# Splitting the last store, moving the last wait to Pool and making do with 14 fewer semaphores in a streaming matrix-vector kernel

## The chip, the cores and the metric

One core of one Trainium2 chip. The metric is the device time of one execution in microseconds (us). The engines are called PE (TensorE, the matrix engine), DVE (VectorE), ACT (ScalarE), Pool (GpSimd) and SyncE. A semaphore is a counter on which engines wait. The traces show a DMA increment one behind its data: in the profiled run of before, the last store's packets ended at 627.520 us, and the last eight increments of its semaphore came from 627.618 to 627.870. A single run of this kernel varies by some 0.2 to 0.3 us (one standard deviation) around its mean.

## The reference

```python
def reference(x, w):                       # x: (8, 2048, 4096) fp32, w: (4096, 1)
    proj = (x @ w).squeeze(-1)             # 8 x 2048
    cm = np.maximum.accumulate(proj, axis=1)
    is_record = (proj >= cm).astype(np.float32)
    return np.cumsum(is_record, axis=1).astype(np.float32)
```

268 MB are read and 64 KB written.

## The kernel before

SyncE issues all loads of x. DVE multiplies and sums 2816 of the 4096 columns of a row, Pool and ACT the other 1280, PE turns the sums into rows of a PSUM tile, and DVE scans them: running maximum, comparison, running count. The sequence of 2048 is done in groups of 512, 512, 512 and 384, and the last 128 positions in a finer tail. The counts stand in `cnt`: one row for each of 8 batches, so partitions 0 to 7.

The parts that matter here:

```python
    xs = [sem("xs") for _ in range(B)]
    fr = [sem("fr") for _ in range(B)]
    xq = [sem("xq") for _ in TILES]                      # 13, one for each load of the tail
    ws, bw, wc, cs, ..., go, ..., ml = (sem(n) for n in ...)   # 19 more
    # ... the loads of the tail: 13 DMAs on SyncE, each .then_inc(xq[i], 16)
    # ... dot(...)._wait_ge(xq[i], 16); G.tensor_mul(...)._wait_ge(xq[i], 16)
        tail_scans(3, 4, 10)                             # the last scan, .then_inc(cs, 1)
        SY.dma_start(out=out[:, STARTS[-1] :], in_=cnt)._wait_ge(cs, NG + 4).then_inc(
            oe, 16
        )
        A.wait_ge(oe, 16)
```

The last store carries 512 columns: 384 of the last group, which are ready some 20 us earlier, and the tail's 128. At the end of the program, outside the kernel's own code, SyncE collects a signal from every engine (its last instruction of this at 628.140 us in the profiled run of before), a barrier follows, Pool clears a range of semaphores (628.627 to 628.958, with records for 54 of them), and a second barrier ends it (629.253).

Of the kernel before, what the change touches and what calls it, by code (L numbers as in the profile page):

```python
# [20 lines left out]
def kernel(  # L21
# [17 lines left out]
    B, S, D = x.shape  # L39
    WC = 512  # L40
    NW = D // WC
# [3 lines left out]
    NG = len(RS)  # L45
    NL = NG - 1
    N = R * P
    STARTS = [sum(RS[:g]) * P for g in range(NG)]
    S0 = sum(RS) * P
# [18 lines left out]
    def rows_of(m):  # L68
        return m * H % B, m * H // B * Q

    TILES = [(m, 0, D, (0, VC), (VC, D)) for m in range(B - 2)] + LAST
# [7 lines left out]
    def sb(shape, name, **kw):  # L79
        return pool.tile(shape, FP32, name=name, **kw)  # L80
# [8 lines left out]
    cnt = sb([B, N], "cnt")  # L89
# [21 lines left out]
    def sem(name):  # L111
        return tc.alloc_semaphore(f"{name}_{next(ns)}")

    xs = [sem("xs") for _ in range(B)]
    fr = [sem("fr") for _ in range(B)]
    xq = [sem("xq") for _ in TILES]
    ws, bw, wc, cs, od, oe, psr, pd, pl, go, sd, pa, con, fo, ms, p7, mg, pg, ml = (
        sem(n) for n in "ws bw wc cs od oe psr pd pl go sd pa con fo ms p7 mg pg ml".split()
    )

    V, A, G, T, SY = nc.vector, nc.scalar, nc.gpsimd, nc.tensor, nc.sync

    def dot(xsl, wsl, dst, seed=0.0):
        return V.tensor_tensor_reduce(  # L124
            out=xsl, in0=xsl, in1=wsl, scale=1.0, scalar=seed,
            op0=ALU.mult, op1=ALU.add, accum_out=dst,
        )

    def add_up(xsl, dst):
        return A.activation(out=xsl, in_=xsl, func=ACTF.Copy, accum_out=dst)  # L130

    def w_pool(c0, c1):
        if c0 >= VC:
            return w_sb[:, c0 - VC : c1 - VC]
        assert W2 <= c0 and c1 <= W2 + W2C
        return w2[:, c0 - W2 : c1 - W2]
# [13 lines left out]
    def at(g, t):  # L150
        return xbuf[(t if g < NL else t + NS - 1) % NS]

    def user_before(g, t):
        if t >= NS:
            return t - NS, g + 1
        if g == NL:
            return B - NS + t, g
        return max(u for u in range(B) if u % NS == t), g

    def free(u, n):  # L160
        return (p7, n) if u == B - 1 else (fr[u], 2 * n)

    with tc.tile_critical(no_gpsimd_drain=True):

        for g in range(NG):
            r = RS[g]
            for t in range(B):
                i = SY.dma_start(
                    out=at(g, t)[:, : r * D],
                    in_=x[B - 1 - t, STARTS[g] : STARTS[g] + r * P, :].rearrange(  # L170
                        "(p r) d -> p (r d)", r=r
                    ),
                ).then_inc(xs[t], 16)
                u, n = user_before(g, t)
                if n:
                    i._wait_ge(*(free(u, n)))
                if g == t == 0:
                    A.dma_start(
                        out=w_row, in_=w.rearrange("(k c) one -> k (c one)", k=NW)
                    ).then_inc(ws, 16)  # L180
                if t == 4 and g:
                    SY.dma_start(
                        out=out[:, STARTS[g - 1] : STARTS[g]], in_=cnt
                    )._wait_ge(cs, g + 1).then_inc(od, 16)

        def slot(m):
            if m < NS:
                return None, xbuf[m][:, RS[-1] * D :]
            u = B - NS if m < 2 * NS else B - NS + 1
            return u, at(NL, u)[:, (m % NS) * D : (m % NS + 1) * D]  # L190
# [3 lines left out]
        for i, (m, c0, c1, _, _) in enumerate(TILES):  # L194
            u, xb = slot(m)
            d = SY.dma_start(  # L196
                out=xb[:, c0:c1],
                in_=x[
                    rows_of(m)[0] : rows_of(m)[0] + H,
                    S0 + rows_of(m)[1] : S0 + rows_of(m)[1] + Q, c0:c1,  # L200
                ].rearrange("b i d -> i b d"),
            ).then_inc(xq[i], 16)
            if u not in freed:
                freed.add(u)
                d._wait_ge(*free(u, NG))
# [4 lines left out]
            out=identity, in_=identity, compare_op=ALU.not_equal, fill=1.0,  # L210
# [10 lines left out]
        for n, k in enumerate(order):  # L221
            c = k * WC
            dst = w_v[:, c : c + WC] if c < CV else ps
            i = T.matmul(  # L224
                out=dst, lhsT=identity[:NW, k : k + 1].to_broadcast([NW, P]),
                rhs=w_row, start=True, stop=True,
            ).then_inc(bw, 1)
# [11 lines left out]
            out=by_b, in_=identity.rearrange("p (i b) -> p b i", b=H),  # L239
# [3 lines left out]
            out=by_i, in_=identity.rearrange("p (i b) -> p i b", b=H), op=ALU.add,  # L243
# [82 lines left out]
        def sums(i, dst_v, dst_p, seed=0.0):  # L326
            nonlocal nv, npool, na
            m, _, _, v, p = TILES[i]
            xb = slot(m)[1]
            dot(xb[:, v[0] : v[1]], w_v[:, v[0] : v[1]], dst_v, seed)._wait_ge(  # L330
                xq[i], 16
            ).then_inc(sd, 1)
            nv += 1
            if p:
                xl = xb[:, p[0] : p[1]]
                G.tensor_mul(out=xl, in0=xl, in1=w_pool(*p))._wait_ge(  # L336
                    xq[i], 16
                ).then_inc(pl, 1)
                npool += 1
                add_up(xl, dst_p)._wait_ge(pl, npool).then_inc(pa, 1)  # L340
                na += 1
# [20 lines left out]
        def tail_scans(k0, k1, base):  # L362
            c = S0 - STARTS[-1]
            a, b = k0 * Q, k1 * Q
            scans(
                cm[:, c + a : c + b], cnt[:, c + a : c + b], ps[:B, a:b],
                cm[:, c + a - 1 : c + a], cnt[:, c + a - 1 : c + a], base,
            )

        for m in range(B - 2):  # L370
            k = m // 2
            v, p = acc_v[:, m : m + 1], acc_p[:, m : m + 1]
            sums(m, v, p)
            pick_a(col(2 * k, m), p)
            pick(G, col(2 * k + 1, m), v)._wait_ge(sd, nv).then_inc(mg, 1)
            if m == 2:
                group_scans(RS[-1])
            if m == 4:
                tail_scans(0, 2, 4)
            if m % 2:  # L380
                if k != 1:
                    T.wait_ge(cs, NG + 1 + k // 2)
                turn(2 * k, k, True, False)._wait_ge(ms, m + 1)
                mm = turn(2 * k + 1, k, False, True)._wait_ge(mg, m + 1)
                if k:
                    mm.then_inc(psr, 1)

        npart = [0, 0]
        for i in range(B - 2, len(TILES)):
            n = i - (B - 2)  # L390
            m, p = TILES[i][0], TILES[i][4]
            z = m - (B - 2)
            v, dp = part_v[:, n : n + 1], part_p[:, n : n + 1]
            s = SEED[n]
            if s is not None:
                V.wait_ge(sd, B - 2 + s + 1)
            sums(i, v, dp, 0.0 if s is None else part_v[:, s : s + 1])
            if p:
                pick_a(col(6 + npart[z], m), dp)
                npart[z] += 1  # L400
            if n in (1, len(LAST) - 2):
                pick(G, col(8, m), v)._wait_ge(sd, nv).then_inc(mg, 1)
            if n == 1:
                tail_scans(2, 3, 7)
# [5 lines left out]
        turn(8, 3, False, False)._wait_ge(mg, B)  # L410
        turn(9, 3, False, True)._wait_ge(ml, 1).then_inc(psr, 1)
        tail_scans(3, 4, 10)
        SY.dma_start(out=out[:, STARTS[-1] :], in_=cnt)._wait_ge(cs, NG + 4).then_inc(
            oe, 16
        )
        A.wait_ge(oe, 16)


# [28 lines left out]
```

## Time and profile before

| | before |
|---|---|
| time, first set | 630.23 us median of 3 (630.13 to 630.26) |
| DMA | 427 GB/s over the span, busy almost throughout |
| engines busy | DVE 65%, Pool 59%, ACT 29%, PE 5% |
| last store issued, in the profiled run | 626.394 us |
| end of the span | 629.253 us |

The profile shows a DMA row of 9s in 39 of 40 slices, and the engines wait for the loads: 181.8 us of idle time ahead of DVE's sums and 243.3 us ahead of Pool's products end on them. So I take the kernel as bound by its loads, and what lies ahead of the first load and behind the last one is left. The lines that carry this stand in the prediction below. I call the time from the issue of the last store to the end of the span the *tail end*: 629.253 - 626.394 = 2.859 us.

### The profile page before, as it was taken

The numbers are of one execution on the slowest core, as the hardware profiler recorded it, in microseconds if no ns is written. First come the engines' busy times: TensorE is split into PE (matmuls) and PEld (weight loads), VectorE is DVE, ScalarE is ACT, GpSimd is POOL, SyncE is SP. The second block draws the span as 40 slices with busy tenths as digits, with TensorE's granted clock in tenths as the row PEclk, the third lists the DMA queues.
The fourth block names the chain that finished last, engine by engine and source line by source line (L and its number), as shares of the span: only waits on it lengthen the run. The fifth ranks groups of instructions, "written<-read, shape, count | busy, mean of one in ns | idle before, by whom it ended". The sixth has DMA issues, their size and how long they took to land. (4 is left out here: it accounts for less than half of the span.)

```text
span 629.3 us, 1140 instructions
## 1 busy us (share of the span) xinstructions
PE 29.1 (5%) x96; PEld 13.5 (2%) x96; DVE 407.3 (65%) x294; ACT 181.2 (29%) x274; POOL 370.7 (59%) x149
## 2 busy tenths in 40 slices
PE   8000000000020000000001000000002000000100
PEld 3000000000010000000000000000001000000000
DVE  0755775556766567755578655676556976655897
ACT  1222332223322233222233222332223232232254
POOL 0554675456765557745577555676557666555775
PEclk9999999999999999999996555555555555555565
DMA  9999999999999999999999999999999999999996
GB/s 401 400 467 400 446 421 425 442 437 429 442 425 450 417 450 417 459 408 458 408 458 408 458 408 458 408 459 408 462 418 438 416 447 441 413 447 444 404 425 248
DMA packets 6563, 268.54 MB, mean 427 GB/s; under 512 B 760, under 2 KB 1016, under 8 KB 1568
## 3 DMA queue, kind: packets, MB, share of 16 engines
q1 hardware_dynamic: 6544, 268.50, 98.9%
q10 hardware_dynamic: 16, 0.02, 0.0%
q14 instruction: 3, 0.02, 0.0%
HBM read 268.45 MB, written 0.07 MB: 427 GB/s over the span
## 5 line engine op out<-in xcount | busy, mean ns | idle before, releaser
L124 DVE CUSTOM_DVE_ANT_0 xall<-xall,w_v 128x2816 f32<-128x2816 f32 (+1 forms) x129 | 385.5, 3041 | 181.8 <-DMA xall<-in_x_dram 181.8
L276 POOL TENSOR_TENSOR xall<-xall,w_sb 128x1280 f32<-128x1280 f32 x120 | 345.0, 2909 | 246.7 <-DMA xall<-in_x_dram 243.3
L130 ACT ACTIVATE xall<-xall 128x1280 f32<-128x1280 f32 (+2 forms) x130 | 162.9, 1253 | 428.6 <-POOL xall L276 408.3
L312 PE MATMUL ps<-identity,small 128*8 128x128 f32 x60 | 13.0, 406 | 568.6 <-PEq L309 568.6
L130 ACT ACTIVATION_READ_ACCUMULATOR xall<-xall 128x1 f32 x130 | 24.2, 186 | 0.0
L336 POOL TENSOR_TENSOR xall<-xall,w_sb 128x1280 f32<-128x1280 f32 (+2 forms) x8 | 21.1, 2632 | 3.1 <-DMA xall<-in_x_dram 3.0
L312 PEld LDWEIGHTS ps<-identity,small 128*8 128x8 f32 x60 | 7.3, 125 | 575.4 <-issue 571.3
L140 DVE TENSOR_TENSOR_SCAN cm<-ps,cm,small 8x512 f32<-8x512 f32 (+3 forms) x8 | 7.0, 869 | 18.8 <-PE ps L312 18.4
L224 PE MATMUL w_v<-w,identity 8*128 8x512 f32 x14 | 12.1, 1056 | 0.0
L124 DVE DVE_READ_ACCUMULATOR2_ANT small<- 128x1 f32 x133 | 10.8, 81 | 0.0
L246 DVE MEMSET ps<- 8x512 f32 x1 | 0.5, 485 | 15.7 <-ACT w L235 15.7
L146 DVE TENSOR_TENSOR_SCAN cnt<-ps,cnt,small 8x512 f32<-8x512 f32 (+3 forms) x8 | 7.0, 870 | 0.3
L224 PEld LDWEIGHTS w_v<-w,identity 8*128 8x128 f32 x14 | 4.6, 332 | 7.3 <-issue 7.3
L143 DVE TENSOR_TENSOR ps<-ps,cm 8x512 f32<-8x512 f32 (+3 forms) x8 | 3.9, 487 | 0.3
L232 ACT COPY w_sb<-w_v 128x768 f32<-128x768 f32 x1 | 0.8, 799 | 11.4 <-PE w_v L224 11.4
L347 POOL TENSOR_TENSOR masked<-fold,small 128x4 f32<-128x4 f32 x8 | 1.6, 201 | 3.2 <-DVE small L124 3.2
L124 DVE CUSTOM_DVE_ANT_0 xall<-xall,w_v,small 128x480 f32<-128x480 f32 (+2 forms) x4 | 3.1, 810 | 0.2 <-DVE small L124 0.2
L357 PE MATMUL ps<-fold,masked 128*8 128x32 f32 x20 | 2.0, 235 | 25.3 <-ACT masked L352 17.7
L352 ACT ACTIVATE masked<-fold,small 128x4 f32<-128x4 f32 x10 | 3.0, 298 | 0.3
L336 POOL TENSOR_TENSOR xall<-xall,w 128x640 f32<-128x640 f32 (+1 forms) x2 | 2.3, 1137 | 0.1
L224 PE MATMUL ps<-w,identity 8*128 8x512 f32 x2 | 2.1, 1135 | 2.6 <-DMA w<-in_w_dram 2.6
L231 ACT ACT_TABLE_LOAD x1 | 1.3, 1283 | 2.7 <-DVE fold L242 2.7
(18 smaller groups left out, 5.3 us busy)
## 6 DMA issues: line engine op xcount, KB each, us to landing
xall<-in_x_dram SPq DMA_DIRECT2D x8, 6144.0 KB, 33.5
xall<-in_x_dram SPq DMA_DIRECT2D x6, 2048.0 KB, 42.4
xall<-in_x_dram SPq DMA_DIRECT2D x1, 1264.0 KB, 36.6
xall<-in_x_dram SPq DMA_DIRECT2D x1, 816.0 KB, 39.3
xall<-in_x_dram SPq DMA_DIRECT2D x1, 784.0 KB, 37.9
xall<-in_x_dram SPq DMA_DIRECT2D x2, 240.0 KB, 26.6
xall<-in_x_dram SPq DMA_DIRECT2D x1, 416.0 KB, 39.4
xall<-in_x_dram SPq DMA_DIRECT2D x24, 45.0
```

The costliest lines, as they stand in the source:

```text
L124: return V.tensor_tensor_reduce(out=xsl, in0=xsl, in1=wsl, scale=1.0, scalar=seed, op0=ALU.mult, op1=ALU.add, accum_out=dst,)
L130: return A.activation(out=xsl, in_=xsl, func=ACTF.Copy, accum_out=dst)
L140: V.tensor_tensor_scan(out=cm_, data0=src, data1=low, initial=cm0, op0=ALU.max, op1=ALU.max,)._wait_ge(psr, base).then_inc(psr, 1)
L143: V.tensor_tensor(out=src, in0=src, in1=cm_, op=ALU.is_ge)._wait_ge(psr, base + 1).then_inc(psr, 1)
L146: V.tensor_tensor_scan(out=cnt_, data0=src, data1=low, initial=cnt0, op0=ALU.add, op1=ALU.max,)._wait_ge(psr, base + 2).then_inc(cs, 1)
L224: i = T.matmul(out=dst, lhsT=identity[:NW, k : k + 1].to_broadcast([NW, P]), rhs=w_row, start=True, stop=True,).then_inc(bw, 1)
L276: i = G.tensor_mul(out=xl, in0=xl, in1=w_sb).then_inc(pl, 1)
L312: i = T.matmul(out=ps[:B, j : r * P : r], lhsT=l[:, j * B : (j + 1) * B], rhs=identity, start=k == 0, stop=k == 1,)
L336: G.tensor_mul(out=xl, in0=xl, in1=w_pool(*p))._wait_ge(xq[i], 16).then_inc(pl, 1)
L347: return eng.tensor_tensor(out=e, in0=by_b, in1=acc.to_broadcast([P, H]), op=ALU.mult)
L352: return A.activation(out=e, in_=by_b, func=ACTF.Copy, scale=acc)._wait_ge(pa, na).then_inc(ms, 1)
L357: return T.matmul(out=ps[:B, k * Q : (k + 1) * Q], lhsT=masked[:, n * B : (n + 1) * B], rhs=by_i, start=start, stop=stop,)
```

## The change

The intent is to shorten that tail end in three ways. The group's 384 columns get a store of their own, issued behind the last load; only the tail's 512 bytes a row are left for the end. Pool instead of ACT waits for the stores, with an increment of a semaphore nobody waits for any more. The tail's 13 loads signal on semaphores that other parts are done with, and the unused `go` is dropped, so that 14 fewer exist.

```diff
-    xq = [sem("xq") for _ in TILES]
-    ws, bw, wc, cs, od, oe, psr, pd, pl, go, sd, pa, con, fo, ms, p7, mg, pg, ml = (
+    ws, bw, wc, cs, od, oe, psr, pd, pl, sd, pa, con, fo, ms, p7, mg, pg, ml = (
...
+    xq = [(ws, 32), (bw, NW + 16), (wc, 3 + 16), (con, 7 + 16), (fo, 1 + 16)]
+    xq += [(s, 32) for s in xs[:5]] + [(s, 2 * NG + 16) for s in fr[:3]]
...
-            ).then_inc(xq[i], 16)
+            ).then_inc(xq[i][0], 16)
...                                      # the two waits on xq[i] take *xq[i]
-        SY.dma_start(out=out[:, STARTS[-1] :], in_=cnt)._wait_ge(cs, NG + 4).then_inc(
-            oe, 16
-        )
-        A.wait_ge(oe, 16)
+        for a, b, n in ((STARTS[-1], S0, 1), (S0, S, 4)):
+            SY.dma_start(
+                out=out[:, a:b], in_=cnt[:, a - STARTS[-1] : b - STARTS[-1]]
+            )._wait_ge(cs, NG + n).then_inc(oe, 16)
+        G.wait_ge(oe, 32).then_inc(ml, 1)
```

More of the change, by code (lines that the diff above doesn't have):

```diff
@@ L115 @@
     fr = [sem("fr") for _ in range(B)]
-    xq = [sem("xq") for _ in TILES]
-    ws, bw, wc, cs, od, oe, psr, pd, pl, go, sd, pa, con, fo, ms, p7, mg, pg, ml = (
-        sem(n) for n in "ws bw wc cs od oe psr pd pl go sd pa con fo ms p7 mg pg ml".split()
-    )
+    ws, bw, wc, cs, od, oe, psr, pd, pl, sd, pa, con, fo, ms, p7, mg, pg, ml = (
+        sem(n) for n in "ws bw wc cs od oe psr pd pl sd pa con fo ms p7 mg pg ml".split()
+    )
+    xq = [(ws, 32), (bw, NW + 16), (wc, 3 + 16), (con, 7 + 16), (fo, 1 + 16)]
+    xq += [(s, 32) for s in xs[:5]] + [(s, 2 * NG + 16) for s in fr[:3]]
     V, A, G, T, SY = nc.vector, nc.scalar, nc.gpsimd, nc.tensor, nc.sync
@@ L330, in sums @@
             dot(xb[:, v[0] : v[1]], w_v[:, v[0] : v[1]], dst_v, seed)._wait_ge(
-                xq[i], 16
+                *xq[i]
             ).then_inc(sd, 1)
@@ L336, in sums @@
                 G.tensor_mul(out=xl, in0=xl, in1=w_pool(*p))._wait_ge(
-                    xq[i], 16
+                    *xq[i]
                 ).then_inc(pl, 1)
```

## The prediction

> **What bounds the kernel now.** I read the page first, then the chain that ended last in order of time, then the timeline and the waits of the last 30 us, and last the semaphore records behind the final instruction, because the change touches nothing else.
>
> ```profile
> DMA  9999999999999999999999999999999999999996
> HBM read 268.45 MB, written 0.07 MB: 427 GB/s over the span
> ```
>
> Over 39 of the 40 slices the 16 DMA engines are at least 90% busy with loading x. The kernel is bound by its loads; a change that neither adds nor removes loads can only act in front of the first or behind the last one. The same shows in stages:
>
> ```profile
> 604.50:622.00 17.50, 1.14 (x12) 0.64 (x12) 15.66 (x19) 7.78 (x18) 13.68 (x10) 0.50 0.99 419
> 622.00:626.40 4.40, 0.87 (x8) 0.41 (x8) 3.90 (x14) 1.97 (x7) 1.82 (x3) 0.50 0.21 81
> 626.40:629.30 2.90, 0.00 (x0) 0.00 (x0) 0.00 (x0) 0.00 (x0) 0.00 (x0) 0.50 0.03 6
> ```
>
> Each line is a window in us with the busy time of PE, PEld, DVE, ACT and Pool, then granted clock, DMA share and GB/s. Until 622 the DMA share is 0.99; for 4.4 us the last sums and scans run; in the last 2.9 us no engine computes at all. Those 2.9 us are where this change must earn what it earns. The end of the chain, and what the queue of SyncE waited for:
>
> ```profile
> 581.81 39.25 DMA xall<-in_x_dram
> 621.06 0.07 issue
> 621.13 1.76 POOL xall L336
> ...
> 626.10 0.27 DVE cnt L146
> ```
> ```profile
> 604.68 1.00 DVE L146 TENSOR_TENSOR_SCAN cnt<-ps,cnt,small 8x384 f32<-8x384 f32 x1
> ...
> 626.39 0.32 SPq L413 DMA_DIRECT2D out_dram<-cnt  x1
> ```
> ```profile
> SPq L413 <- DVE cnt L146: 21.8, 1, 21.8
> ```
>
> 384 of the 512 columns that the last store carries are ready at 604.68 + 1.00 = 605.68, but their store waits until 626.39 for the tail's last scan; SyncE sits idle 21.8 us. Behind the store stand only waits and the clean-up:
>
> ```profile
> L163 ACTq COMPARE_BRANCH  x1: 37/37/37, 627.9 to 627.9; - x1
> L163 ACTq DRAIN  x1: 8/8/8, 628.1 to 628.1; - x1
> L163 SPq NOP  x1: 13/13/13, 628.1 to 628.1; - x1
> ```
> ```profile
> L442 POOLq EVENT_SEMAPHORE_RANGE_CLEAR  x1: 331/331/331, 628.6 to 628.6; - x1
> L442 POOLq EVENT_SEMAPHORE  x4: 17/17/17, 628.3 to 629.1; - x4
> ```
>
> ACT holds the wait for the store (a branch that waits), then tells SyncE, whose NOP closes the collection; Pool then clears the range of semaphores in 331 ns, and a second barrier ends the program at 629.25.
>
> The trace's own records give these steps to the nanosecond. Issue 626.394 (319 ns); eight data packets of 2048 bytes from 627.183 to 627.520, which took 107, 227, 234, 111, 233, 211, 81 and 81 ns; increments of the store's semaphore: one at 626.872, eight from 627.618 to 627.870. ACT's branch 627.891, its drain 628.062, SyncE's NOP 628.140, clear 628.627 to 628.958, last semaphore instruction ended 629.253. So: store 1.476 us (626.394 to 627.870), hand-over 0.270 us (627.870 to 628.140), barrier before the clear 0.487, clear 0.331, rest 0.295.
>
> [...] This store is issued by SyncE, not GpSimd; here the receipt part is 627.870 - 627.520 = 0.35 us and issue to first packet is 0.79 us, so the larger piece lies in front of the data. Either way bytes are the small part of 1.476 us.
> [...]
> [...] SyncE's last load issue ends at 604.54 by the timeline; no run yet shows a store behind the tail loads.
> [...] ACT's waiting branch to ACT's next instruction is 171 ns, of which 37 are recorded, while two successive semaphore instructions of Pool start 78 ns apart (628.310 and 628.388).
>
> **The change part by part.**
> (1) Two stores for one. The first, 8 x 1536 bytes, needs the group's scan (605.68) and is issued about 605.7, in SyncE's idle time. A 2048-byte packet of the three earlier stores took 84 ns under full load, so this one is about 65 ns on each of eight engines, behind the last load, whose packets end at 622.9 (623.75 on the slowest engine). It should land by about 624.2, over 3 us before the second. On the path: 0. The second store has 512 instead of 2048 bytes a row. Load packets of 1920 and 3328 bytes took 79 and 131 ns, so 0.037 ns a byte; 1536 bytes fewer is 57 ns. The packets of 211 to 234 ns carry some 140 ns that isn't bytes at this rate; I leave it in place. Worth -57 ns; -130 if the slow packets shrink in proportion.
> (2) The wait moves from ACT to Pool, and the built program shows how. On ACT the wait sits on the branch that leaves the critical part. On Pool it increments a semaphore, so it stays an instruction of its own, and the branch behind it has no wait; such branches leave no record in this trace (Pool, DVE and PE have none at the place of ACT's). New path: landing, about 21 ns to Pool's wait (as ACT's, 627.870 to 627.891), 78 ns to Pool's NOP, about 22 for its increment (626.802 to 626.824), about 20 until SyncE's NOP, which is the last of SyncE's collecting instructions and waits for Pool alone. ACT was collected one instruction earlier; that hop goes. Sum 141 ns for 270: -129 ns. Pool's drain of 41 ns moves behind its NOP, but the barrier needs SyncE's increment 146 ns after SyncE's NOP (628.140 to 628.286), so it stays hidden.
> (3) The 13 semaphores of the tail's loads (one for each entry of the list of tail tiles, 6 + 7) and the unused `go` are no longer made: 14 fewer. The clear covered 48 of the kernel's and 6 of the frame's, 54, as its records count; after, 40. Its records run from 628.648 to 628.930, 5.3 ns each; 14 x 5.3 = 74. Clear 331 to 257: -74 ns.
> (4) The reused semaphores change only the numbers waited for: no instruction, no order. The instruction order agrees on all engines but for one more store on SyncE and Pool's wait. 0.
> Sum: -57 - 129 - 74 = -260 ns; 630.23 - 0.26 = 629.97 us, 0.04%.
>
> **The rivals.**
> A: the early store collides with the last loads and pushes the tail. For it: those loads do set the chain (39.25 us of it)[...]. Against it: [...] even wholly in front it adds only 65 ns to eight engines. It would give 630.0 to 630.1.
> B: the store is latency alone: fewer bytes save nothing, or the smaller row pays the same slow packets. For it: 0.79 and 0.35 us of 1.476 are not data, and half of the packets were slow while nothing else ran. Then 630.03.
> C: Pool's hand-over isn't shorter, because its branch costs something though unrecorded, as ACT's does (171 against 78 ns). Then (2) gives about -40 (the hop alone), 630.06.
> D: a wait on a reused semaphore ends late or early, and the tail's DVE or Pool stalls. The counts are exact multiples reached before the tail's landings, and the race check passes; it would show as idle time from 604 on. Under 5% for me; some us.
> A gain of 2% would be 12.6 us, four times the whole idle end.
>
> **Range and chances.** The parts together can give from -0.1 (B and C) to -0.35 (slow packets shrink), so 629.88 to 630.13. Three runs of before spread over 0.13, and its profiled run took 631.05; another session can shift by some tenths. I say 629.96, with 629.65 to 630.2 for 8 in 10. Within 2%: 0.99; faster and slower 0.005 each.
>
> **What would show it.** (1) A store issue at about 605.7, and a last one at 626.4 with packets of 512 bytes that end some 60 ns sooner. (2) No waiting branch on ACT; landing to SyncE's NOP about 140 ns. (3) A clear of about 257 ns. All engines' rows until 626.4 as before. A last load landing later, or a span that shrinks by over 0.4 us or not at all, would make me wrong in mechanism, though hardly in the verdict.

The forecast's sum came to -57 - 129 - 74 = -260 ns. That the early store would come behind the loads was the assumption. The "about 20" of part (2) is an estimate that names no source; the trace after has 17 ns there.

## The result, and the profile after

The changed kernel took 629.65 us (median of 4, 629.52 to 629.75), before 630.25 (median of 4, 630.13 to 630.47). The ratio is 0.999 with a 95% interval from 0.9973 to 1.0007. A ratio here is the mean time of one kernel's runs over that of the other's of the same rounds, so not quite the ratio of the medians. The interval holds 1: these eight runs alone don't show a gain. The medians differ by 0.60 us where I had said 0.26, and 629.65 lies at the very edge of my range. By the 2% line it is the same, as predicted; the size was wrong.

First the loads and the end of the chain, in order of time (start, length, what):

```profile
580.85 39.27 DMA xall<-in_x_dram
620.12 0.07 issue
620.19 1.76 POOL xall L338
...
625.14 0.27 DVE cnt L148
```

All of it comes 0.96 us earlier than before, but no part is shorter: 39.27 us of loads for 39.25, and 625.14 - 580.85 = 44.29 for 626.10 - 581.81 = 44.29. So the early store did not disturb the loads, and the 0.96 arose far ahead of anything that was changed: the chain's first piece, at 483 us, already comes 0.96 us earlier. The profiled run of before had taken 631.05 us, slower than its others; one must not read a gain from two single spans.

Stages after, in windows as for before (us, busy time of PE, PEld, DVE, ACT and Pool, granted clock, DMA share, GB/s):

```profile
622.00:625.43 3.43, 0.86 (x8) 0.41 (x8) 2.93 (x12) 1.87 (x6) 0.93 (x2) 0.50 0.04 14
625.43:627.80 2.37, 0.00 (x0) 0.00 (x0) 0.00 (x0) 0.00 (x0) 0.00 (x0) 0.50 0.01 2
```

The stretch in which nothing computes has shrunk from 2.9 to 2.4 us. Its parts, first the queue of SyncE, then the collection, then the clear:

```profile
604.76 20.97 SPq L416 DMA_DIRECT2D out_dram<-cnt  x2
```
```profile
L165 ACTq DRAIN  x1: 8/8/8, 625.8 to 625.8; - x1
...
L165 POOLq NOP  x1: 13/13/13, 626.8 to 626.8; - x1
L165 SPq NOP  x1: 13/13/13, 626.8 to 626.8; - x1
```
```profile
L445 POOLq DRAIN  x3: 34/41/103, 626.9 to 627.6; - x3
L445 POOLq EVENT_SEMAPHORE_RANGE_CLEAR  x1: 248/248/248, 627.3 to 627.3; - x1
```

Two stores now share one line of this answer, from 604.76 to the end of the second's issue. The early store's own issue took 3.10 us, against 0.30 of the last one; SyncE had nothing else to do. ACT is through its part at 625.8, 0.4 us after the start of the last store's issue for 1.7 before, Pool's NOP is the last to be collected, and the clear has fallen from 331 to 248 ns. The trace's records, in ns (the store runs from the start of its issue to the last increment of its semaphore; the NOP is SyncE's last instruction of the collection; the rest is the second barrier):

| | before | after | difference | predicted |
|---|---|---|---|---|
| last store, issue to last increment | 1476 | 1235 | -241 | -57 |
| hand-over, increment to SyncE's NOP | 270 | 165 | -105 | -129 |
| barrier, NOP to clear | 487 | 460 | -27 | 0 |
| clear | 331 | 248 | -83 | -74 |
| rest | 295 | 295 | 0 | 0 |
| tail end | 2859 | 2403 | -456 | -260 |

The early store's packets started 17.0 to 18.0 us after its issue, the last of them at 622.808, where the last packet of the loads had ended at 622.806: it did wait for the loads, as the prediction had assumed. Its last increment came at 623.336, 2.1 us ahead of the last store's issue. So 0.46 of the 0.60 us are accounted for by the tail end, the store is the large miss, and 0.14 us are open. The experiments go to these two.

### The profile page after: what moved, and what is told of

Its sections match the earlier page's. It is cut to its first block, busy times and chain, and to the rows that moved or that the text cites. A ratio compares the mean times of both kernels' runs of the same rounds, so it can differ in the third digit from the quotient of the medians.

```text
span 627.8 us, 1141 instructions
## 1 busy us (share of the span) xinstructions
PE 29.4 (5%) x96; PEld 13.6 (2%) x96; DVE 407.2 (65%) x294; ACT 181.1 (29%) x274; POOL 370.5 (59%) x149
```

## The experiments

All numbers of a tail end are ns from the run's own trace. Times are means of five runs against the nine of before in the same set, unless said otherwise.

### Each part alone, and all together

The store alone, with the wait left on ACT's branch:

```diff
-        SY.dma_start(out=out[:, STARTS[-1] :], in_=cnt)._wait_ge(cs, NG + 4).then_inc(oe, 16)
-        A.wait_ge(oe, 16)
+        for a, b, n in ((STARTS[-1], S0, 1), (S0, S, 4)):
+            SY.dma_start(out=out[:, a:b], in_=cnt[...])._wait_ge(cs, NG + n).then_inc(oe, 16)
+        A.wait_ge(oe, 32)
```

> Only the split of the last store; the wait stays on ACT's branch, the semaphores stay 54. Theory S (the eight rows of a store share one rate of about 48 GB/s, as 16384 bytes in 0.337 us before and 4096 in 0.086 after say): last issue to last increment falls from 1.476 to about 1.24 us, time -0.24 us against before. Theory P of the prediction (each packet pays its own 0.037 ns a byte): -0.06, at most -0.13. Hand-over stays 0.27 us and the clear 331 ns under both.

The wait alone:

```diff
-        A.wait_ge(oe, 16)
+        G.wait_ge(oe, 16).then_inc(ml, 1)
```

> Only the wait moved to Pool, with its increment; one store of 2048 bytes a row, 54 semaphores. Prediction: landing to SyncE's NOP 0.141 us for 0.270, time -0.13; the changed kernel's trace had 0.165, so -0.11 is the better guess. Rival C (Pool's branch costs though unrecorded): 0.23 us or more, time -0.04 or less. Store stays about 1.48 us, clear 331 ns.

The semaphores alone: the changed kernel with the old store and the old wait put back.

> Only the 14 semaphores fewer (the tail's loads on reused ones); one store, wait on ACT. Prediction: clear about 250 ns for 331, time -0.08, nothing else. Rival F (the 0.14 us of the measured 0.60 that the tail's 0.46 do not hold come from reused semaphores somewhere in front of the last store): time about -0.22, and the issue of the last store comes earlier.

And the whole change once more:

> The whole change again, in the same rounds as its parts. If the parts add up and theory S holds: -0.24 -0.11 -0.08 = -0.43 us, near the 0.46 of the tail in the first trace. If the 0.60 of the first medians is real throughout: -0.6, and the three parts must leave 0.15 over or one of them be larger than its place in the tail shows. Theory P: -0.26.

| | store | hand-over | barrier | clear | tail end | against 2859 | mean time against before |
|---|---|---|---|---|---|---|---|
| store alone | 1227 | 270 | 486 | 331 | 2609 | -250 | -0.40 us |
| wait alone | 1474 | 165 | 485 | 331 | 2751 | -108 | -0.25 us |
| semaphores alone | 1472 | 270 | 460 | 248 | 2746 | -113 | -0.22 us |
| all | 1237 | 164 | 460 | 248 | 2404 | -455 | -0.54 us |

In the traces the parts separate cleanly: each moves its own columns and no other, and -250 - 108 - 113 = -471 is the -455 of all but for 16 ns. The store alone varies by about as much between traces: 1227 to 1245 ns with 512 bytes a row. Theory S is borne out (-249 ns expected about -240), and the prediction's price for the bytes falls. The -0.027 of the barrier belongs to the semaphores. But the mean times of all four lie 0.08 to 0.15 us lower than their tail ends explain. The semaphores' -0.22 us is what rival F of their expectation forecast; the nulls further down show offsets of this size without any change.

### Where the store's time was

Before, the eight packets of 2048 bytes started over 230 ns and took 81 to 234 ns each; after, eight of 512 bytes took 25 to 34. From first start to last end that is 16384 bytes in 337 ns, 48.6 GB/s, and 4096 bytes in 86 ns, 47.6 GB/s: two very different sizes at one common rate. The early store is a hint too: its eight packets of 1536 bytes, from the same partitions but with starts spread over 1.07 us, took 65 ns each, none of them longer. Either the rows share something at their source (theory S1) or at their destination (S2). This pair of kernels gives a wrong result on purpose: the store reads eight rows of another tile of the same width, once from every fourth partition, once from partitions 0 to 7. (That every fourth would keep the rows apart was the assumption.)

```diff
-        SY.dma_start(out=out[:, STARTS[-1] :], in_=cnt)...
+        SY.dma_start(out=out[:, STARTS[-1] :], in_=w_sb[: 4 * B : 4, :N])...   # every fourth
+        SY.dma_start(out=out[:, STARTS[-1] :], in_=w_sb[:B, :N])...            # 0 to 7, the control
```

> Wrong result on purpose: the last store takes its eight rows of 2048 bytes from partitions 0, 4, ... 28 of another tile (the broadcast weights) instead of 0 to 7 of the counts. Theory S1 [...] each packet takes 81 to 110 ns, first packet to last end falls from 0.337 to 0.15-0.19 us, last issue to last increment from 1.476 to about 1.30. Theory S2 (the shared limit is on the side of the destination in HBM): unchanged, 0.33 and 1.47.

> Wrong result on purpose: control of the run before; the same other tile, rows of 2048 bytes from partitions 0 to 7. Both theories: as before, data 0.33 us, packets up to 234 ns, issue to last increment 1.47. If it differs from before, the tile and not the partitions matters.

The rate of the DMA in windows of 1.2 us that hold the last store, in 40 slices of 30 ns; first the control, then every fourth partition, then the changed kernel with its 512 bytes a row:

```profile
GB/s 0 0 0 0 0 0 205 68 68 0 68 68 0 69 0 0 0 0 0 0 0 0 0 0 0 0 0 0 0 0 0 0 0 0 0 0 0 0 0 0
```
```profile
GB/s 0 0 0 0 0 0 0 341 137 68 1 0 0 0 0 0 0 0 0 0 0 0 0 0 0 0 0 0 0 0 0 0 0 0 0 0 0 0 0 0
```
```profile
GB/s 0 0 0 0 0 0 0 68 35 35 0 0 0 0 0 0 0 0 0 0 0 0 0 0 0 0 0 0 0 0 0 0 0 0 0 0 0 0 0 0
```

A packet counts here where it starts. With rows 0 to 7 the starts are strung out over eight slices (to the ns: packets of 107, 227, 234, 109, 233, 211, 81 and 81, data 331); with every fourth partition all eight start within 62 ns, each takes 81 ns, and the data are through in 143. The control equals before, so the tile is not the cause, and the destination is the same in both. The limit is at the source: partitions 0 to 7, 331 ns for 143. (The run by fours had a slower issue as well, see below, but its eight packets were in flight together, and none slowed another.) What it is at the source that these rows share, and between which partitions its borders lie, no run here shows.

Spreading the rows is no gain here, though. The same run's issue:

```profile
L413 SPq DMA_DIRECT2D out_dram<-w_sb x1: 756/756/756, 625.8 to 625.8; - x1
```

It took 756 ns for 320, and the first packet came 1391 ns after the start of the issue for 792: the store got 399 ns slower than before (1875 for 1476) and the kernel 0.38 us. I had expected 1300 and had not thought of the issue at all.

The size between, with 256 columns in each store:

```diff
-        for a, b, n in ((STARTS[-1], S0, 1), (S0, S, 4)):
+        for a, b, n in ((STARTS[-1], STARTS[-1] + N // 2, 1), (STARTS[-1] + N // 2, S, 4)):
```

> The whole change, but the early store carries 256 columns and the last one 256 (1024 bytes a row, partitions 0 to 7): the dose between. [...] 8192 bytes take 0.17 us from first packet to last end (0.33 at 2048 a row, 0.09 at 512), last issue to last increment about 1.32; time +0.08 against the whole change. Theory P (0.037 ns a byte for each packet alone): +0.02, 1.255. If only rows of 2048 bytes are slow (a threshold): as the whole change, 1.24.

Data 165 ns, packets 44 to 74, issue to last increment 1308, tail end 2475; mean time -0.48 us against before. 8192 bytes in 165 ns are 49.6 GB/s; the expectation's 0.17 us had been worked out with about 49, from the rates of the two sizes before. So three sizes (86, 165 and 331 to 337 ns) lie near one line, and neither the price for single packets (1255) nor a threshold (1240) holds.

One step further, a third store, so that only 32 columns, 128 bytes a row, are left:

```diff
-        for a, b, n in ((STARTS[-1], S0, 1), (S0, S, 4)):
+        for a, b, n in ((STARTS[-1], S0, 1), (S0, S - Q, 3), (S - Q, S, 4)):
...
-        G.wait_ge(oe, 32).then_inc(ml, 1)
+        G.wait_ge(oe, 48).then_inc(ml, 1)
```

> The whole change with three stores: 384 columns behind the last load, 96 columns when the third scan of the tail is done (about 620.2), 32 columns at the end: 128 bytes a row. Theory S: data time is 4096 bytes at 48 GB/s = 0.086 us now, 0.02 at 1024 bytes but for the 0.06 us over which the eight packets start; last issue to last increment 1.20 for 1.236, time -0.03. [...]

Correct, and the shortest tail end of all: 2340 ns. The packets took 11 ns each, the data 71 (60 of them the spread of the starts), issue to last increment 1172 for 1235. Of these 63 ns the issue itself gave some: the first packet came 752 ns after its start for 781, which I had not expected. Short rows carried no extra time: packets that did not share took 11 ns at 128 bytes, 22 at 384, 25 at 512 and 65 at 1536, so 6 to 8 ns and 0.037 ns a byte throughout. The mean time was 629.82, -0.52 us against before; the step beyond the whole change rests on the trace, as 64 ns can't be seen in five runs.

### Which part of the hand-over

The traces show a bare wait on the branch that follows it (a COMPARE_BRANCH holds it: ACT's in before, 37 ns at 627.891 us), while a wait with an increment is an instruction of its own (Pool's EVENT_SEMAPHORE after, 17 ns at 626.694). Engine and form can be crossed, with all else as in the whole change:

```diff
-        G.wait_ge(oe, 32).then_inc(ml, 1)
+        G.wait_ge(oe, 32)                      # Pool, bare
+        A.wait_ge(oe, 32).then_inc(ml, 1)      # ACT, with the increment
```

> The whole change with Pool's wait left bare, without the increment of a semaphore: the wait goes onto Pool's branch, as ACT's did. Prediction's reading: the branch costs what ACT's did (171 ns to the next instruction for 100 of Pool's semaphore instruction), landing to SyncE's NOP 0.23-0.24 us for 0.165. If the engine is what matters and not the branch: 0.165.

> The whole change with the wait on ACT and the increment kept, so that it is an instruction of its own on ACT. If the branch is the cost and the hop small: ACT's next instruction starts 80-100 ns after the wait, and the collection's one instruction more adds about 40: landing to SyncE's NOP 0.19-0.21 us, between 0.165 (Pool) and 0.270 (ACT's branch). If ACT is slow by itself: 0.25 or more.

Pool's bare wait shows up as the branch:

```profile
L165 POOLq COMPARE_BRANCH  x1: 38/38/38, 626.8 to 626.8; - x1
L165 POOLq NOP  x1: 13/13/13, 626.9 to 626.9; - x1
L165 SPq NOP  x1: 13/13/13, 627.0 to 627.0; - x1
```

| last increment to SyncE's NOP, ns | wait on the branch | wait as its own instruction |
|---|---|---|
| ACT | 270 | 184 |
| Pool | 229 | 165 |

The form is worth 64 to 86 ns and the engine 19 to 41. From the wait to the engine's next instruction it is 171 (ACT) and 167 (Pool) on a branch, 86 and 101 otherwise. The rest of the way is by subtraction 99 and 98 ns with ACT, 62 and 64 with Pool: Pool gains its part where SyncE's collection ends, as SyncE's last instruction waits for Pool and the one before it for ACT (in before that one ended at 628.101 us, 39 ns ahead of the last). ACT's 184 is a little below what I had expected (190 to 210). Most of "Pool holds the last wait" is thus in the increment that looks idle. The mean times were -0.60 and -0.65 us; they can't order the three forms, the traces do.

### Whether the clear counts semaphores

The whole change with 14 semaphores made and never used:

```diff
+    for _ in range(14):
+        sem("un")
```

> The whole change with 14 semaphores allocated and never used. If the semaphores' gain is the clear alone: clear back to 331 ns, and Pool's drain before it back to 128 ns for 103, tail +0.11 against 2.404 (83 ns of the clear, 27 of the barrier). If the drain's 25 ns came from something else in the change: tail +0.08.

```profile
L447 POOLq DRAIN  x2: 34/81/128, 627.7 to 628.3; - x2
L447 POOLq EVENT_SEMAPHORE_RANGE_CLEAR  x1: 331/331/331, 627.9 to 627.9; - x1
```

The clear is back at 331 ns and the drain ahead of it at 128 for 103; tail end 2522, +119 against the first trace after, of which 10 are the store's scatter and 83 + 27 the clear and the barrier. So it is the number of semaphores, not their reuse: 331 ns with 54 of them, 248 with 40, and 83 / 14 = 5.9 ns each. Why the drain, which stands ahead of the clear, grows with their number stays open. The mean time was -0.45 us.

### The open 0.14 us

A kernel that equals before but for a comment:

> The kernel before with one comment line more: a null. All four kernels of the first set ran 0.08 to 0.15 us further below before's mean than their tails explain. If that is chance or the order within a round, this one runs 0.0 to -0.15 us too and its tail (last issue to end) is 2.86 us. If it is a real effect of the changes in front of the last store, this one is within 0.05 of before while the others are not.

It came out at -0.08 us with a tail end of 2859, and the control above, with before's tail end to 2 ns, at -0.18. So the offset showed in kernels with nothing to gain. That is chance, the chip of the set or something in the comparison; two more nulls and two more copies of the whole change in the same rounds, in alternating places, were to tell:

> The kernel before under another comment. If the comparison itself puts everything about 0.1 us below before (its place in a round, or chance in before's runs), this and the second null again come out 0.05 to 0.2 below it; if that was chance in the nulls so far, within 0.05.

> The whole change, against the two nulls of the same rounds instead of against before: 0.46 us below them if the tail holds all of the gain; 0.60 below them if 0.14 us more come from in front of the last store. Ten runs each, with a spread of 0.2 a run, tell these apart only roughly (0.09 of error), so all nulls and all whole changes of the case will be taken together.

> As the first null; if the place within a round matters, the two nulls differ from each other by more than their spread (0.2).

> As the first copy of the whole change, in another place of the round: tail 2.404 us, and 0.46 or 0.60 below the nulls.

| | mean of 5 | against before | tail end, ns |
|---|---|---|---|
| null A | 630.36 | +0.17 | 2854 |
| whole change A | 630.07 | -0.13 | 2409 |
| null B | 630.42 | +0.23 | 2861 |
| whole change B | 629.83 | -0.37 | 2413 |

This time the nulls lie above before, so a kernel that is not before does not always come out lower, and the two nulls, in different places of the round, agree within 0.06: before's own mean moves by 0.1 to 0.3 us from set to set (630.27, 630.42, 630.34, 630.54, 630.20), whether by chance or by chip. The two copies together are 629.95, the two nulls 630.39: 0.44 us, and the tail ends differ by 2857.5 - 2411 = 446 ns. 40 runs of before average 630.36, 15 runs of nulls 630.35 and 19 of the whole change 629.87, a difference of 0.49 with an error of 0.07 (from the spreads of the runs). That agrees with 0.46; 0.60 is 1.5 errors away. Without the first set, whose surplus is in question, the difference is 0.44 with an error of 0.08, and 0.60 is almost two errors away: unlikely, though not excluded. The last store's issue, too, lay anywhere from 625.28 to 626.39 in traces of kernels whose front is the same. So the runs give no sign of a gain in front of the last store.

## Why the prediction was right or wrong, point by point

*What bounds the kernel*, *no collision of the early store* (rival A; of the reasons against it only the 65 ns stand, the other is cut) and *reused semaphores cost nothing* (rival D) were right: the chain from the last tail loads to the last scan is equal to 0.01 us, the early store's packets took the 65 ns that had been said, and the semaphores alone moved nothing but barrier and clear.

*Part 1 failed, and it is the term that was mis-sized.* "0.037 ns a byte; 1536 bytes fewer is 57 ns" took the price of a packet from full-width loads and let each of the eight packets pay it alone; it measured 241 to 250 ns. I had the contradiction on the table: packets of one size took from 81 to 234 ns with nothing else running. I wrote that the extra 140 ns of the slow packets "isn't bytes at this rate" and left it in place, where it was the bytes of the other rows from the same partitions, 0 to 7. 12288 bytes fewer at 49 GB/s are 250 ns. The alternative "-130 if the slow packets shrink in proportion" pointed the right way and was still half of it; the packets also start sooner after one another (over 60 ns for 230). The prediction's own sign of a wrong mechanism, a span that shrinks by over 0.4 us, came true: the tail end shrank by 0.456. Rival B, that the store is latency alone, is refuted by the same runs; the pieces that are not data hardly moved (issue to first packet 0.789 us before and 0.781 after, last packet to last increment 0.350 and 0.368).

*Part 2* was right in what it named (the form of the wait was worth 64 to 86 ns, the engine 19 to 41) and high by 24 ns (-129 for -105): from Pool's wait to its next instruction it took 101 ns, not 78. The pair is 23 ns slower than the two successive semaphore instructions it was priced by. Whether the branch between, which leaves no record, is the cause (this much of rival C would then be true) is not shown.

*Part 3* was right for the clear (-83 for -74); it missed the 27 ns of the barrier ahead of it, 25 of them in Pool's drain.

The sum: -0.26 predicted, and -0.184 (store), -0.009 (clear), -0.027 (barrier) and +0.024 (hand-over) give the -0.456 of the tail end. The first four runs' median fell further, to 629.65, but over 19 runs the changed kernel's mean is 629.87: as far as the runs show, the last 0.2 us of that median were chance. The range of 8 in 10 was laid around a sum with one term four times too small; its lower end, given as -0.35, is -0.33 by the prediction's own terms.

## What to carry to other kernels

Price a small store from few partitions by where its rows lie: here eight rows in partitions 0 to 7 shared one rate of 48 to 50 GB/s (81 to 234 ns a packet, for 81 from every fourth partition), and equal packets with unequal times said so before any experiment. When a change is smaller than the scatter of the runs, divide the trace behind the last common event into its steps and compare those, and run a null before explaining what is left. A wait at the end of a program may ride on a branch; in this kernel an increment that nobody needs kept it off, for 64 to 86 ns.
